# Seven stage joints of one long block: the order of some steps changed

## The chip, the cores and the metric

The kernel runs on one core of one Trainium2 chip. The metric is the time of one execution on the device in microseconds; a kernel is timed in several runs, and their median stands for it. Everything is one program with one launch. One further execution was recorded by the hardware profiler, and all rows below are from it.

## The reference

Two transformer-like blocks on one sequence of 1024 positions and 1024 channels, all in fp32. The first block, cut to what matters:

```python
h = rmsnorm(x, g_mix); z = h @ w_in
a = layernorm(causal_dwconv(a_val * sigmoid(a_gt), 31 taps))   # long branch
y_a = silu(a) @ w_a_out
s = sc_b * causal_dwconv(sc_c * sc_v, 3 taps)                  # short branch
y_b = s @ w_b_out
x = x + (sigmoid(gate_a) * y_a + sigmoid(gate_b) * y_b) @ w_o
u = rmsnorm(x) @ w_up                                          # 2 x 2816 columns
x = x + (gelu(causal_dwconv(u_gate, 3 taps)) * u_value) @ w_down
x = x + sigmoid(rmsnorm(x) @ w_ple_gate) * (p @ w_ple)
```

It ends with a norm. The second block modulates and projects the result again, runs latent attention with four heads and a context of 256 positions, a pooling branch, two gated products and an output projection.

## The kernel before, in words

Activations lie with channels on the 128 partitions and positions along the free axis: a [1024, 1024] activation is eight tiles of 128x1024, each in two halves of 512 columns (h = 0, 1). To hold fp32 accuracy every operand is split into a high and a low part of a shorter format (`split`, `load_w`): ScalarE copies the high part, VectorE or GpSimd subtracts it to get the low part. A product is then three matmuls (`mm3`, lines 138 to 140: high by high, low by high, high by low) that add up in one of eight accumulator banks. `gemm` does this over the input tiles: 24 matmuls for one half of a weight column with eight tiles, 48 for both.

All is written as one straight program; the framework places tiles in pools, inserts the waits and plans the order of each engine's queue, using the program order as priority. So an engine's order is fixed before the run, and may differ from the text. Pools matter here: `slot` has 32 tiles of 128x1024; `half_t` 8 tiles of 128x512; weights have 5 raw buffers and 3 each for high and low; there are 8 banks.

A norm's scale is made in three steps (class `Stats`): squares are added over the tiles; `rstd` sums them over the partitions with small matmuls (line 186) and makes the reciprocal root on VectorE in a chain of small steps, then writes it on the diagonals of four 128x128 blocks (`diag`, line 201); `spread` multiplies a matrix of ones with these diagonals (line 207), which puts the scale on all partitions, and ScalarE copies it out (line 208). TensorE's queue stands at the spread until the diagonal is there.

Stages around the change, in order:

- Short branch. Four tiles `sv` are made and split into `sp_`. Then for each j of 8, `gate(8 + j)` (48 matmuls, two multiplications by the scale `rb` at line 570, a sigmoid), the product "yb" with `w_b_out` (24 matmuls for both halves), a multiplication of the two at line 586, and a store. Between these stand steps of the long branch's convolution, taken from a queue `bgq` by `bg(n)`: it runs up to n steps and stops at a `None`. Then eight more gates follow with `bg(3)` after each half, during which the LayerNorm of the long branch runs from the same queue (`ln_sum`, `ln_mean`, `ln_center`, `ln_sq`, `ln_rstd`, `ln_spread`, `ln_out`).
- Mix and w_o. The loop over h and j of 8 adds the product with `w_o` to x (line 675) and gathers the second norm's squares; for h = 1 it makes the scale of the first half, after j = 2, and spreads it, after j = 4, into `rb2`.
- FFN up. 22 tiles of 128 gate and 128 value columns. Each is made by a scheme of seven products of 12 matmuls (`a0, b0, b1, t1 to t4`) on sums of blocks, instead of eight. `quad_first` does the first tile; `begin(j)` loads the weights of tile j, makes their sums on GpSimd and issues product a0; `quad(j)` does the rest. The result `ug` goes through `ff_conv` (convolution, gelu), is multiplied with the value part in `ff_end` and stored in `f_spill`. The operands of the seven products take 28 slots through all of this.
- FFN down. `load_f` reads a stored tile back and splits it; the 22 tiles come in chunks of 3, 8, 6 and 5 (`FF_CHUNKS`). In the last chunk the loop over h and d of 8 also gathers the third norm's squares; for h = 1 it makes the first half's scale after d = 3 and spreads it into `rb3` after d = 5. Steps of an unrelated matrix-vector product (`mod_step`) run on VectorE from `bgq`.
- PLE. Products "pg" and "ple", the latter with small weights `ws`; the scaled result is split into `hB`.
- Second block. The first gate columns "ga": two weights are loaded, both first halves multiplied, then `norms2(1)` (line 186 sums and a reciprocal root), one second half, `norms2_spread(1)`, the other second half.

## Time and profile before

| | us |
|---|---|
| median of 3 runs | 1999.13 |
| lowest, highest | 1996.34, 2002.65 |
| the profiled execution | 1998.57 |
| its span, first to last instruction | 1996.8 |

How to read what follows: PE is TensorE's matmuls, PEld its weight loads, DVE VectorE, ACT ScalarE, POOL GpSimd, SP the queue of SyncE that issues most DMAs; a "q" behind an engine's name is its queue issuing a DMA. L12 is line 12 of the kernel. An operand is written out<-in by the program's names; a name ending in h or l is a high or low part. The square bracket at the end of a row is the engine's idle time just before and what ended it. A matmul is listed longer than it holds the engine: the next starts before it ends. [...]

### The profile page before, as it was taken

The page shows a single profiled execution, that of the slowest core. Times are in us where ns is not written, and L with a number is a line of the kernel's source. Part 1 is how long each engine was busy: PE and PEld are TensorE (multiplying, and loading weights), DVE is VectorE, ACT ScalarE, POOL GpSimd, SP SyncE. Part 2 cuts the span into 40 slices and gives each one's busy share as a digit, 9 for nine tenths or more (in the row PEclk, how much of TensorE's full clock was granted, in tenths as well). Part 3 has the DMA queues.
Part 4 walks back from the last instruction along what each step waited for, and adds up shares of the span by engine and source line. Part 5 has one row for each costly group of instructions (what it writes and reads, how often), then busy time and mean ns, then how long its engine had stood idle before and what let it go on. Part 6 is the DMA issues. An engine that isn't in the chain of part 4 may idle for free.

```text
span 1996.8 us, 24031 instructions
## 1 busy us (share of the span) xinstructions
PE 1944.2 (97%) x8958; PEld 1581.6 (79%) x8958; DVE 1457.3 (73%) x2219; ACT 705.3 (35%) x1172; POOL 591.1 (30%) x417
## 2 busy tenths in 40 slices
PE   9999989999999999999999999999999999999999
PEld 7888768778877777777777777878778878888887
DVE  6798679356668888888884539986888476878751
ACT  6210221233344333333334322345442256556510
POOL 1334522130012445454541010223354322323200
PEclk9999989999999999999999999999999999999999
DMA  6011122113442222222224535534331221001141
GB/s 216 32 43 38 63 77 76 58 40 108 147 140 89 72 87 70 89 69 90 69 92 166 203 113 191 173 133 147 121 117 55 72 87 35 14 14 43 44 183 48
DMA packets 76612, 186.11 MB, mean 93 GB/s; under 512 B 8784, under 2 KB 15568, under 8 KB 76496
## 3 DMA queue, kind: packets, MB, share of 16 engines
q1 hardware_dynamic: 68000, 162.04, 24.3%
q10 hardware_dynamic: 8496, 22.55, 2.9%
q8 instruction: 70, 1.15, 0.2%
q14 instruction: 46, 0.38, 0.1%
HBM read 149.42 MB, written 35.13 MB: 92 GB/s over the span
## 4 chain that ended last, share of the span: by engine, by line
PE 75%; DVE 12%; issue 6%; ACT 4%; POOL 2%; DMA 1%; ACTq 0%; DVEq 0%; SPq 0%; POOLq 0%
PE q L138 4%; PE wd L139 4%; PE wd L140 4%; PE wd L138 3%; PE q L139 3%; PE q L140 3%; PE gate L139 3%; PE gate L138 3%; PE gate L140 3%; DVE fa L335 2%; PE pv L1338 2%; PE wo L138 2%; PE wout L140 1%; PE wout L139 1%; PE wo L139 1%
## 5 line engine op out<-in xcount | busy, mean ns | idle before, releaser
L133 ACT ACTIVATE wh<-wr 128x1024 fp32r<-128x1024 f32 (+2 forms) x116 | 115.6, 998 | 353.6 <-PE wd L139 90.2
L134 POOL TENSOR_TENSOR wl<-wr,wh 128x1024 fp32r<-128x1024 f32 x44 | 119.8, 2724 | 276.0 <-ACT wh L133 264.4
L156 DVE TENSOR_TENSOR wl<-wr,wh 128x1024 fp32r<-128x1024 f32 (+1 forms) x92 | 159.8, 1737 | 49.7 <-ACT wh L155 49.6
L335 DVE SCALAR_TENSOR_TENSOR acc<-av,vec,acc 128x1023 f32<-128x1023 f32 (+14 forms) x120 | 186.5, 1554 | 10.2 <-ACT acc L344 7.5
L155 ACT ACTIVATE wh<-wr 128x1024 fp32r<-128x1024 f32 (+1 forms) x92 | 86.6, 942 | 205.5 <-issue 137.0
L138 PE MATMUL q<-t,wh 128*128 128x512 f32 x352 | 141.9, 403 | 5.1 <-DVE qm L700 4.7
L139 PE MATMUL wd<-fl,wh 128*128 128x512 f32 x352 | 139.3, 397 | 1.3 <-DVE fl L782 1.2
L139 PE MATMUL q<-t,wh 128*128 128x512 f32 x352 | 139.2, 396 | 0.2 <-DVE t L156 0.2
L140 PE MATMUL q<-t,wl 128*128 128x512 f32 x352 | 139.1, 395 | 0.0
L140 PE MATMUL wd<-fh,wl 128*128 128x512 f32 x352 | 138.5, 395 | 0.0
L138 PE MATMUL wd<-fh,wh 128*128 128x512 f32 x352 | 134.4, 403 | 3.8 <-ACT fh L781 3.8
L225 POOL TENSOR_TENSOR ss<-ss,sq 128x512 f32<-128x512 f32 x42 | 61.8, 1487 | 203.6 <-ACT sq L224 203.6
L138 PE MATMUL gate<-hh,wh 128*128 128x512 f32 x256 | 102.1, 399 | 0.0
L139 PE MATMUL gate<-hl,wh 128*128 128x512 f32 x256 | 101.0, 395 | 0.0
L140 PE MATMUL gate<-hh,wl 128*128 128x512 f32 x256 | 100.5, 393 | 0.0
L134 DVE TENSOR_TENSOR wl<-wr,wh 128x1024 fp32r<-128x1024 f32 (+2 forms) x72 | 83.7, 1162 | 16.4 <-ACT wh L133 15.1
L138 PEld LDWEIGHTS q<-t,wh 128*128 128x128 f32 x352 | 66.3, 188 | 29.2 <-DVE qm L700 13.2
L759 POOL TENSOR_TENSOR fa<-fa,rb 128x1024 f32<-128x1024 f32 x22 | 53.6, 2436 | 120.3 <-ACT fa L758 120.3
L1313 POOL TENSOR_SCALAR wr<-wr,rsum 128x1280 f32<-128x1280 f32 x32 | 42.9, 1341 | 145.8 <-DVE rsum L1312 131.2
L138 PEld LDWEIGHTS wd<-fh,wh 128*128 128x128 f32 x352 | 66.7, 190 | 21.0 <-ACT fh L781 5.1
L139 PEld LDWEIGHTS wd<-fl,wh 128*128 128x128 f32 x352 | 66.6, 189 | 19.2 <-DVE fl L782 3.3
L140 PEld LDWEIGHTS wd<-fh,wl 128*128 128x128 f32 x352 | 66.5, 189 | 15.8
(466 smaller groups left out, 5486.8 us busy)
## 6 DMA issues: line engine op xcount, KB each, us to landing
wr<-in_w_upq SPq DMA_DIRECT2D x88, 256.0 KB, 3.0
wr<-in_w_in SPq DMA_DIRECT2D x32, 512.0 KB, 3.3
wm<-in_w_modT SPq DMA_DIRECT2D x48, 256.0 KB, 3.0
f_spill<-fa ACTq DMA_DIRECT2D x22, 512.0 KB, 2.6
fl<-f_spill SPq DMA_DIRECT2D x22, 512.0 KB, 5.7
x<-in_xT SPq DMA_DIRECT2D x32, 256.0 KB, 4.5
wr<-in_w_o SPq DMA_DIRECT2D x16, 512.0 KB, 3.2
x_spill<-x ACTq DMA_DIRECT2D x32, 256.0 KB, 2.0
```

The costliest lines, as they stand in the source:

```text
L133: S.activation(out=hi, in_=raw, func=AF.Copy)
L134: lo_eng.tensor_tensor(out=lo, in0=raw, in1=f32(hi), op=ALU.subtract)
L138: PE.matmul(ps, lh, rh, start=start, stop=False, **kw)
L139: PE.matmul(ps, lh, rl, start=False, stop=False, **kw)
L140: PE.matmul(ps, ll, rh, start=False, stop=stop, **kw)
L155: S.activation(out=hi, in_=src, func=AF.Copy)
L156: V.tensor_tensor(out=lo, in0=src, in1=f32(hi), op=ALU.subtract)
L225: eng.tensor_tensor(out=self.sums[:, hs(h)], in0=self.sums[:, hs(h)], in1=q, op=ALU.add)
L335: V.scalar_tensor_tensor(out=acc[:, s:T], in0=src[:, 0 : T - s], scalar=w, in1=acc[:, s:T], op0=ALU.mult, op1=ALU.add)
L759: G.tensor_tensor(out=fa, in0=fa, in1=rb2, op=ALU.mult)
L1313: G.tensor_scalar(out=pm, in0=pm, scalar1=rs, scalar2=1.0, op0=ALU.mult, op1=ALU.mult)
L1338: PE.matmul(self.pv, v4[cc][x], y[:, cc, :], start=b + n + cc == 0, stop=b == 4 and n == 2 and cc == 1)
```

## The change

Seven edits, all of order.

- In LayerNorm's part of the queue, `ln_rstd` stands one place earlier: it runs after the half gate that follows the last `ln_sq`, not after the next. `ln_spread` keeps its place.
- `gate(8)` is issued before the loop over j, and each turn issues `gate(9 + j)` before its own product. Products and gates stay the same.
- The spread into `rb2` of the first half moves from after j = 4 to after j = 6.
- The spread into `rb2` of the second half, with the scaling and convolution of FFN tile 0, moves out of the place behind `begin(1)` into a function `first_tile`, which `quad(1)` calls behind its product t2.
- The `load_f` of the first chunk's three tiles stand before the last FFN tile's `quad(21)` instead of after its `ff_end`.
- The spread into `rb3` of the first half moves from after d = 5 to after d = 7.
- At the start of the second block three gate weights are taken instead of two; `norms2(1)` follows three first halves, and its spread two second halves.

```diff
-    bgq.extend([None, ln_rstd, None, ln_spread, None])
+    bgq.extend([ln_rstd, None, None, ln_spread, None])
...
+    ahead = deque([gate(8)])
     for j in range(KD):
-        g = gate(8 + j)
+        if j < KD - 1:
+            ahead.append(gate(9 + j))
+        g = ahead.popleft()
         bg(4)
...
-            if h and j == 4:
+            if h and j == 6:
                 st.spread(rb2, (0,))
...
         product(y, w, "t2")
+        if callable(prev):
+            prev = prev()
         padd(u2, y, m1)
...
-    ug = slot("ug")
-    cs = quad_first(wq0, ug)
+    ug0 = slot("ug")
+    cs0 = quad_first(wq0, ug0)
     nxt = begin(1)
-    st.spread(rb2, (1,))
-    V.tensor_tensor(out=ug, in0=ug, in1=rb2, op=ALU.mult)
-    prev = 0, ff_conv(0, ug), cs
-    for j in range(1, N_FF):
-        ug, cs, nxt = quad(j, *nxt, prev)
-        prev = j, ff_conv(j, ug), cs
-    ff_end(*prev)
+
+    def first_tile():
+        st.spread(rb2, (1,))
+        V.tensor_tensor(out=ug0, in0=ug0, in1=rb2, op=ALU.mult)
+        return 0, ff_conv(0, ug0), cs0
...
+    fs = {}
+    prev = first_tile
+    for j in range(1, N_FF):
+        if j == N_FF - 1:
+            for k in range(FF_CHUNKS[0]):
+                fs[k] = load_f(k)
+        ug, cs, nxt = quad(j, *nxt, prev)
+        prev = j, ff_conv(j, ug), cs
+    ff_end(*prev)
...
         for k in range(j0, j0 + n):
-            fs[k] = load_f(k)
+            if ci:
+                fs[k] = load_f(k)
...
-            if h and d == 5:
+            if h and d == 7:
                 st.spread(rb3, (0,))
...
-    w = [load_w(a["w_fm"][i], KD, lo_eng=G) for i in range(2)]
-    bs = [bias_col(w[i]) for i in range(2)]
-    gs = [[gemm(w[i], hB[0], None, "ga")] for i in range(2)]
+    w = [load_w(a["w_fm"][i], KD, lo_eng=G) for i in range(3)]
+    bs = [bias_col(w[i]) for i in range(3)]
+    gs = [[gemm(w[i], hB[0], None, "ga")] for i in range(3)]
     norms2(1)
     gs[0].append(gemm(w[0], hB[1], None, "ga"))
+    gs[1].append(gemm(w[1], hB[1], None, "ga"))
     norms2_spread(1)
-    gs[1].append(gemm(w[1], hB[1], None, "ga"))
+    gs[2].append(gemm(w[2], hB[1], None, "ga"))
     for i in range(2):
         ga_evict(i, bs[i], gs[i])
-    g = ga_gemm(2)
     next(ctx_parts)
     load_tm(0)
     load_tm(1)
-    ga_evict(2, *g)
+    ga_evict(2, bs[2], gs[2])
```

## Rows read from the trace of the kernel before

**Rows 1.** The page: busy time of TensorE and its weight loads, among all engines.
```profile
PE 1944.2 (97%) x8958; PEld 1581.6 (79%) x8958; DVE 1457.3 (73%) x2219; ACT 705.3 (35%) x1172; POOL 591.1 (30%) x417
```
**Rows 2.** Waits of TensorE: who <- whom: us in total, times, longest.
```profile
PE sp L207 <- DVE dg L201: 10.6, 5, 4.2
PE yb L139 <- DVE spl L156: 5.1, 2, 4.6
...
PE wd L138 <- ACT fh L781: 3.8, 3, 3.1
```
**Rows 3.** Windows: stretch, length, busy (x count) per engine; PEclk, DMA share, GB/s; products yb.
```profile
245.40:263.40 18.00, 9.88 (x26) 6.50 (x25) 15.59 (x14) 2.73 (x3) 6.43 (x3) 0.62 0.05 15
...
274.50:280.10 5.60, 5.60 (x26) 4.55 (x25) 5.53 (x6) 0.93 (x2) 0.00 (x0) 1.00 0.23 94
```
**Rows 4.** Timeline of TensorE at a spread without a wait: start, us, what.
```profile
1353.53 1.02 PE L207 MATMUL sp<-dg,ones 128*128 128x512 f32 x2
1353.98 0.80 PE L138 MATMUL pg<-h,wh 128*128 128x512 f32 x1
1354.62 0.39 PE L139 MATMUL pg<-h,wh 128*128 128x512 f32 x1
```
**Rows 5.** Windows again: stretches around five of the other waits.
```profile
427.70:433.20 5.50, 2.90 (x8) 1.16 (x7) 4.54 (x11) 1.88 (x3) 2.40 (x1) 1.00 0.29 80
595.10:601.20 6.10, 4.11 (x10) 2.32 (x9) 6.10 (x9) 3.20 (x5) 2.10 (x2) 0.72 0.25 72
640.90:648.90 8.00, 3.81 (x8) 2.11 (x7) 7.83 (x13) 0.60 (x1) 5.03 (x4) 0.79 0.03 10
1064.50:1076.00 11.50, 7.50 (x25) 5.09 (x24) 7.50 (x8) 5.72 (x6) 3.29 (x2) 0.85 0.94 338
1312.00:1317.90 5.90, 4.05 (x10) 2.33 (x9) 5.69 (x13) 2.32 (x3) 1.96 (x2) 0.71 0.46 152
```
**Rows 6.** Timeline of VectorE in the short branch.
```profile
256.14 1.23 DVE L156 TENSOR_TENSOR spl<-sv,sph 128x1024 fp32r<-128x1024 f32 x1
...
285.78 0.69 DVE L570 TENSOR_TENSOR gate<-gate,rb 128x512 f32<-128x512 f32 x1 [2.17 <-PE gate L140]
```
**Rows 7.** Timelines of VectorE and TensorE in LayerNorm.
```profile
404.73 0.68 DVE L225 TENSOR_TENSOR lnv<-lnv,sq 128x512 f32<-128x512 f32 x1
...
431.80 1.12 PE L207 MATMUL sp<-dg,ones 128*128 128x512 f32 x2 [2.33 <-DVE dg L201]
```
**Rows 8.** Timeline of VectorE before the second FFN spread.
```profile
641.36 3.96 DVE L201 TENSOR_SCALAR dg<-ident,rc 128x128 f32<-128x128 f32 x4
645.25 0.68 DVE L700 TENSOR_TENSOR ug<-q,qm 128x512 f32<-128x512 f32 x1
```
**Rows 9.** Timelines of TensorE, SyncE's queue and ScalarE at the last FFN tile.
```profile
1053.31 0.50 PE L138 MATMUL q<-t,wh 128*128 128x512 f32 x1 [0.23 <-DVE qm L700]
...
1058.42 0.42 SPq L780 DMA_DIRECT2D fl<-f_spill  x1
...
1066.69 1.04 ACT L781 ACTIVATE fh<-fl 128x1024 fp32r<-128x1024 f32 x1
```
**Rows 10.** Timelines of VectorE and TensorE from the down stage into PLE.
```profile
1320.40 0.69 DVE L855 TENSOR_TENSOR x<-wd,x 128x512 f32<-128x512 f32 x1 [1.67 <-PE wd L140]
...
1330.20 0.75 DVE L134 TENSOR_TENSOR ws<-wr,ws 128x256 fp32r<-128x256 f32 x2
...
1330.66 0.50 PE L140 MATMUL ple<-pp,ws 128*128 128x512 f32 x1 [0.78 <-DVE ws L134]
```
**Rows 11.** Timeline of TensorE at the sums and spread of the second block.
```profile
1458.70 1.84 PE L186 MATMUL ts<-ones,ss 128*128 128x2 f32 x16
...
1466.07 1.02 PE L207 MATMUL sp<-dg,ones 128*128 128x512 f32 x2
```
**Rows 12.** Timelines of ScalarE, VectorE and TensorE: fourth convolution, first and last step, and the mean.
```profile
297.18 1.23 ACT L344 ACTIVATE acc<-av,vec 128x1024 f32<-128x1024 f32 x1
...
351.65 1.25 DVE L335 SCALAR_TENSOR_TENSOR acc<-av,vec,acc 128x994 f32<-128x994 f32 x1
...
391.09 1.02 PE L376 MATMUL mu<-lns,ones 128*128 128x512 f32 x2
```

More of the change, by code (lines that the diff above doesn't have):

```diff
@@ L789, in block_kernel @@
     j0 = 0
-    fs = {}
     def down(d, h, w, n):
```

## The prediction

> **What bounds the kernel now.** I read the page's busy table first: TensorE is busy for 1944.2 of 1996.8 us [rows 1]. No other engine comes near it, so the time can only fall by closing TensorE's idle time, some 50 us with the head and tail, and the slow matmuls right behind it. The second view is who waited for whom on TensorE [rows 2]: the largest entry is the spread of a norm, which waits for VectorE's diagonal (10.6 us in five waits), then the short branch's product and the first product after the FFN. The third view gives each stretch around such a wait its length, its count of instructions and its granted clock [rows 3, 5]. [...] I therefore price a joint as its stretch less its work at full pace. The pace is 24 matmuls in 5.6 us, 0.23 us each [rows 3]. A spread that waits for nothing costs 0.86 us: from its start at 1353.53 to the next full-pace matmul at 1354.62 are 1.09 us, one matmul included [rows 4]. Counts in the windows include one or two instructions that hang over from before.
>
> **The change part by part.** The ceiling of each, and what I take:
>
> 1. Gate one ahead of the short branch. Now the first product takes 18.0 us where a later one takes 5.6 [rows 3], a loss of 12.4. It waits for VectorE's splits, the last ending at 256.14 + 1.23 = 257.4 [rows 6]. The change puts another gate of 48 matmuls (11.1 us) before it, so the product starts near 256.5 and reaches the matmul that needs this split (the tenth or so) at about 258.6: covered with 1.2 us to spare. The second gate's weights are needed earlier; the trace shows no weight wait of a gate, and three weight buffers allow it. VectorE has a backlog until 285.78, where it first waits for TensorE by 2.17 [rows 6]; meanwhile TensorE, 12.4 us ahead, fills banks: two gates, one product and the next gate make at most 7 of 8 by my count, so no new wait. The price, if the splits move later by more than 1.2 us, is one for one. I take 12.0, bounds 8 to 12.4. All gates and products are merely permuted; the gate is stored and read back long after.
>
> 2. LayerNorm's sums half a gate earlier. The stretch of 5.5 us holds two matmuls and two spreads: 5.5 - 0.5 - 1.7 = 3.3, of which 2.33 is the wait before the second spread [rows 5, 7]. The sums move up by half a gate, 5.6 us, more than the wait. Their input is complete at 404.73 + 0.68 [rows 7], long before. I take 3.0, bounds 2.3 to 3.3.
>
> 3. First norm spread of the FFN two weight columns later (j = 4 to 6). 6.1 us hold six matmuls and one spread: 6.1 - 1.4 - 0.9 = 3.8 [rows 5]. Two columns are 48 matmuls, 11.1 us, so the diagonal is ready with margin. But VectorE then feeds the FFN's first tile, and the x loads, queued on SyncE behind weight loads that wait for VectorE, follow no faster than VectorE. I take 3.0, bounds 1.5 to 3.8.
>
> 4. Second spread behind one more product of the second tile. 8.0 us hold five matmuls and a spread: 8.0 - 1.2 - 0.9 = 5.9 [rows 5]. The moved product (12 matmuls, 2.8 us) goes into this wait, but the diagonal still ends at 641.36 + 3.96 = 645.3 [rows 8]. Moreover the product takes the accumulator bank that the spread has now; all eight are in use, and the next is free when VectorE's addition of 645.25 ends at 645.93 [rows 8]. So 2.8 - 0.6 = 2.2 at most return unless the clock stays up, and VectorE's remaining additions may then be waited for. [...]
>
> 5. First three activations reloaded ahead of the last FFN tile. 11.5 us hold 24 matmuls: 11.5 - 5.5 = 6.0 [rows 5]. The first load is issued at 1058.42 and its split on ScalarE starts at 1066.69, while TensorE has run dry [rows 9]. Named earlier, it has room once the products of the last tile give up operand slots, about a tile (20 us) ahead of TensorE's need. On SyncE it passes ahead of the first down weights; these are held by weight buffers anyhow. Against it: three ScalarE copies and three VectorE subtractions enter the last tile's queues, where TensorE already waits 0.23 us for an addition [rows 9]. If a subtraction of 1.2 us (128x1024, as the split of 256.14 [rows 6]) stands ahead of that addition, TensorE pays it. I take 5.0, one such collision; bounds 2 (three collisions) to 6.0.
>
> 6. Spread after the down product two rows later (d = 5 to 7). 5.9 - 1.4 - 0.9 = 3.6 [rows 5]. Here VectorE is the next bound. Right behind, TensorE waits 0.78 us for the small weights' lower part, which VectorE makes at 1330.20 at the end of a queue with only 1.67 us of idle time at 1320.40 [rows 10]. TensorE comes 3.6 earlier, VectorE can follow by 1.7, so this wait grows by 1.9. I take 3.6 - 1.9 = 1.7, bounds 0 to 3.6.
>
> 7. Third gate weight ahead in the second block. The sums at 1458.70 and the spread at 1466.07 show no idle time before them [rows 11]: nothing waits where the change adds cover. The waits just before are for the previous stage's last splits, which all three first halves still need. One more weight's bias column comes forward on VectorE. I take 0, bounds -1.5 to +1.
>
> Sum: 12.0 + 3.0 + 3.0 + 1.8 + 5.0 + 1.7 + 0 = 26.5. The profiled execution took 1998.57 (span 1996.8), 0.6 below the median of 1999.13; 1998.6 - 26.5 = 1972.1. No instruction is removed or added; all of it is order.
>
> **The rivals.**
>
> A. Every wait closes, and the clock with it: 12.4 + 3.3 + 3.8 + 5.9 + 6.0 + 3.6 = 35.0, giving 1963.6. For it: each edit sits at a measured wait. Against it: parts 4 and 6 have VectorE close behind.
>
> B. The next-late resource takes the place of the waits: parts 3 to 6 return nothing on balance, because diagonals, splits and additions all hang on VectorE; parts 1 and 2 hold: 15.0, giving 1983.6. For it: the diagonal of part 4 and the queue of part 6. Against it: parts 3 and 5 have microseconds of cover.
>
> C. The change does not do what it says. The framework orders each engine's queue by a plan of its own, and reorders across the program text: the reload of part 5 already stands ahead of the last tile's end [rows 9]. The plan may already issue what the text moves, or put the moved work back. Then the waits stay: 1993 to 2002, about 1998.
>
> D. Slower, by one mechanism: tile room. The pool has 32 slots; at the short branch I count 16 for the normalised input, 1 scale, 3 accumulators, 1 or 2 inputs, 8 for the branch's splits, leaving 2 or 3 for gates and the fourth accumulator. The change keeps two gates alive where one was. The fourth convolution starts at 297.18, its last step ends at 352.9, and TensorE needs the resulting mean at 391.09 [rows 12], which becomes 378.7. With three sums of 1.2 us, 22 us are spare. If the second gate held the accumulator's slot until the branch's splits go free (the last product, at 262 + 6 x 11.1 + 7 x 5.6 = 368), the convolution would start 71 us later, TensorE would stand for 71 - 22 = 49, and the time would be 1972 + 49 = 2021. It decides the sign once the start slips beyond about 347. Against it: two slots suffice for two gates, and VectorE's lag, not room, sets the start.
> [...]
>
> **How the numbers follow.** Forecast (1968 to 1980): 0.50. B and mixtures towards it: 0.25. A: 0.12. C: 0.08. D: 0.05. The likeliest time is 1972. The lower bounds of all parts together save 13, the upper ones 36; a range from 1962 to 1987 takes in forecast, A and B, and leaves out C, D and a few hundredths of tails. About 0.3% (6 us) is what a measurement here can tell from no change; faster by more is forecast, A and B together, 0.87; within it is C, 0.08; slower is D, 0.05.
>
> **What would show it.** In the changed profile: the first short-branch product takes about 5.6 us, at clock 1.00; no spread in LayerNorm, FFN entry j or down stage has a wait before it except the second FFN spread, with 1.5 to 2; the first product after the FFN follows the last tile at once; the small-weight wait near the first PLE product grows from 0.8 to nearly 3; nothing changes at the second block's start. The prediction is wrong if a wait of several us stands in the last FFN tile (loads not landed), before the LayerNorm mean (slots), or if the attention stage's order, untouched by the text, comes out otherwise.

## The result, and the profile after

The changed kernel takes 1976.7 us (median of four runs, 1974.2 to 1980.3) against 1999.0 of the kernel before beside it; the ratio is 0.9889, with a 95% interval of 0.9875 to 0.9904. Run again later beside other kernels it took 1979.5 us (1977.3 to 1980.3), a ratio of 0.9898 [0.9883, 0.9913]. The profiled execution took 1974.2 us with a span of 1972.4, 24.4 below the one of before. The forecast was 1972, with a range of 1962 to 1987.

The page of the changed kernel, busy time of all engines, answers to [rows 1]:

```profile
PE 1935.7 (98%) x8958; PEld 1578.8 (80%) x8958; DVE 1457.4 (74%) x2219; ACT 705.9 (36%) x1172; POOL 593.2 (30%) x417
```

The counts are the same as before: nothing was added. TensorE is busy 8.5 us less with the same work, as less of it falls in stretches of a lower granted clock (PEclk, a share of full speed, is 0.997 over the whole span, where it was 0.992; single microseconds of the changed kernel read 1.00 from 1294 to 1300 us and 0.50 from 1301 to 1306). The waits of TensorE in the changed kernel (who <- whom: us in total, times, longest), beside [rows 2]:

```profile
PE q L138 <- DVE qm L703: 7.3, 20, 1.8
...
PE ple L140 <- DVE ws L134: 3.0, 2, 2.3
...
PE ple L138 <- ACT ws L133: 2.6, 1, 2.6
PE sp L207 <- DVE dg L201: 2.3, 1, 2.3
...
PE q L139 <- DVE t L156: 1.0, 2, 0.8
...
PE q L138 <- ACT wh L155: 0.8, 1, 0.8
```

The 10.6 us at spreads have become 2.3, and these are at another spread, the context's at 1482.10. The waits of the short branch's product and of the first down product are gone. New or larger are the small weight of the per-layer embedding (ple), the FFN's additions (qm), among which now stands one of 1.8 us, and the splits for the FFN's first products (t, wh).

To see where the time went I take the start of the same matmul in both traces and compare the lengths of the stretches between. "Again" is the second profile of the changed kernel. Matmuls are counted from 0 among those of one output: wo for the output projection, q for the FFN, wd for its down product, pg for the PLE gate (PLE is the per-layer embedding). All in us; a minus is time lost.

| stretch | before | after | again | saved: after (again) | predicted |
|---|---|---|---|---|---|
| start to the first gate | 234.25 | 234.59 | 234.60 | -0.3 (-0.4) | 0 |
| to LayerNorm's mean | 156.84 | 144.39 | 144.39 | 12.5 (12.5) | 12.0, part 1 |
| to the output projection (matmul 190) | 174.94 | 171.80 | 171.80 | 3.1 (3.1) | 3.0, part 2 |
| to the first FFN matmul | 50.72 | 46.86 | 46.86 | 3.9 (3.9) | with the next |
| to FFN matmul 300 (fourth tile) | 79.07 | 78.27 | 80.25 | 0.8 (-1.2) | 4.8, parts 3 and 4 |
| to FFN matmul 1740 | 343.16 | 343.11 | 343.14 | 0 (0) | 0 |
| to down matmul 60 | 45.60 | 39.92 | 39.92 | 5.7 (5.7) | 5.0, part 5 |
| to down matmul 1024 | 227.08 | 224.22 | 225.69 | 2.9 (1.4) | 0 |
| to PLE gate matmul 48 | 27.81 | 29.65 | 28.36 | -1.8 (-0.6) | 1.7, part 6 |
| to the token-major products (utm) | 208.94 | 210.62 | 212.18 | -1.7 (-3.2) | 0, part 7 |
| to the end | 448.36 | 449.00 | 451.29 | -0.6 (-2.9) | 0 |
| sum, unrounded | | | | 24.4 (18.3) | 26.5 |

Two profiles of one kernel are 6 us apart, and yet half of the rows agree to 0.03 us. So a whole execution says little about an edit worth 2 us; its stretch says much, if it is one of the steady ones. The experiments below are read that way.

Three joints as they stand now. Windows of the changed kernel (stretch, length, busy per engine with counts, granted clock, DMA share, GB/s), the first product of the short branch:

```profile
256.80:262.50 5.70, 5.70 (x26) 4.65 (x25) 5.62 (x6) 1.26 (x3) 0.00 (x0) 1.00 0.00 0
```

It takes 5.7 us at a granted clock of 1.00 where it took 18.0 at 0.62 [rows 3]. Timelines of TensorE, VectorE and GpSimd around the second FFN spread (start, us, what; in brackets idle time before it):

```profile
622.70 0.88 DVE L201 TENSOR_SCALAR dg<-ident,rc 128x128 f32<-128x128 f32 x4
...
627.21 1.02 PE L207 MATMUL sp<-dg,ones 128*128 128x512 f32 x2
...
626.04 1.29 POOL L652 TENSOR_TENSOR wr<-wr 128x512 f32<-128x512 f32 x1 [17.44 <-DVE wl L156]
```

The diagonal of four steps took 3.96 us before [rows 8] and takes 0.88 now. Before, GpSimd's weight additions ran beside it, from 641.35 to beyond its end, 1.3 us each; now they come 2.5 us after it. Timeline of GpSimd before:

```profile
641.35 1.26 POOL L649 TENSOR_TENSOR wr<-wr 128x512 f32<-128x512 f32 x1 [15.76 <-DVE rc L180]
```

The spread has no wait. Timeline of TensorE at the end of the FFN: the first down product follows the last FFN product with no gap, and the last tile's wait is 0.60 us, where 0.23 was normal [rows 9]:

```profile
1033.74 0.50 PE L138 MATMUL q<-t,wh 128*128 128x512 f32 x1 [0.60 <-DVE qm L703]
...
1044.74 0.39 PE L140 MATMUL q<-t,wl 128*128 128x512 f32 x1
1044.97 0.40 PE L138 MATMUL wd<-fh,wh 128*128 128x512 f32 x1
```

### The profile page after: what moved, and what is told of

The parts are those of the page before. It is cut to its first block, busy times and chain, and to the rows that moved or that the text cites. A ratio compares the mean times of both kernels' runs of the same rounds, so it can differ in the third digit from the quotient of the medians.

```text
span 1972.4 us, 24045 instructions
## 1 busy us (share of the span) xinstructions
PE 1935.7 (98%) x8958; PEld 1578.8 (80%) x8958; DVE 1457.4 (74%) x2219; ACT 705.9 (36%) x1172; POOL 593.2 (30%) x417
## 4 chain that ended last, share of the span: by engine, by line
PE 43%; DVE 12%; issue 5%; ACT 4%; POOL 1%; DMA 1%; DVEq 0%; SPq 0%; ACTq 0%; POOLq 0%
PE q L138 3%; PE wd L139 3%; PE wd L140 3%; PE wd L138 3%; PE q L140 3%; PE q L139 3%; DVE fa L335 2%; PE pv L1351 2%; PE wout L138 2%; PE wout L140 2%; PE wout L139 1%; PE pg L138 1%; PE pg L140 1%; PE pg L139 1%; PE pT L1340 1%
## 5 line engine op out<-in xcount | busy, mean ns | idle before, releaser
L138 PEld LDWEIGHTS q<-t,wh 128*128 128x128 f32 x352 | 66.0, 188 | 33.1 <-DVE qm L703 16.5
L139 PEld LDWEIGHTS q<-t,wh 128*128 128x128 f32 x352 | 66.1, 188 | 16.9 <-DVE t L156 1.9
```

The lines of the kernel that those rows point to most:

```text
L138: PE.matmul(ps, lh, rh, start=start, stop=False, **kw)
L139: PE.matmul(ps, lh, rl, start=False, stop=False, **kw)
```

## The experiments

Unless said otherwise the diffs are against the changed kernel, and a run is one profiled execution. The names of the second block: ga are its gate products; pin the products of its pooling branch (the expectations call them pinned); between these stand the parts of the context, which are its sums, its spread, its product uc (with the low part hcl) and a transposition ckTc; utm are the token-major products, kv the first products of the attention.

**The first part alone.** The kernel before, with only the gate drawn ahead.

```diff
+    ahead = deque([gate(8)])
     for j in range(KD):
-        g = gate(8 + j)
+        if j < KD - 1:
+            ahead.append(gate(9 + j))
+        g = ahead.popleft()
```

> The kernel before with the first of the edits alone: one gate ahead of the short branch's product. Theory (the wait was for VectorE's splits, and nothing downstream gives the time back): the first product takes 5.7 us instead of 18.0, TensorE reaches the LayerNorm mean 12.4 us earlier than before, and the whole is 12.4 +- 1 shorter than the kernel before (profiled span near 1984.4). Rival (two gates alive take tile room, later stages absorb part): under 9 us at the end, with a wait in the long branch's convolution or at the mean.

It took 1988.1 us (span 1986.3). From the first gate to the mean it needs 144.39 us, the same to 0.01 as the whole change: 12.45 us are this part's alone. The stretches to the FFN are as before (174.95, 50.75). The span is 10.5 shorter than that of before, which neither theory named: 1.0 us is lost ahead of down matmul 60, and 2.2 us at the context's first product, in a stretch that no edit touches, by a wait that the trace of before does not have:

```profile
PE uc L140 <- DVE hcl L520: 1.8, 1, 1.8
```

**The third part undone** (first FFN spread back at column 4).

```diff
-            if h and j == 6:
+            if h and j == 4:
                 st.spread(rb2, (0,))
```

> The changed kernel with the FFN's first spread put back after j = 4. Theory 1 (the start of the FFN is paced by VectorE's chain of differences, splits and additions, so that the two spread edits share one limit): the spread waits some 2 us again, TensorE enters the FFN 3.8 us later, but by the fourth FFN tile only 0 to 2 us of that are left, and the end is 0 to 2 later than the changed kernel (span 1972.4 to 1974.5). Theory 2 (the edits add up): 3.8 later at the fourth tile and at the end, span 1976.2.

It took 1977.2 us. The entry to the FFN is 50.71 us again, as before (50.72). From the output projection to FFN matmul 300 it needs 128.8 us; the ten profiles with both parts need 125.1 (the changed kernel's first) to 127.4, so the part is worth 1.4 to 3.7 us there, 2.6 by their mean. At the end the run is 3.05 us behind the first profile and 3.0 ahead of the second. That does not decide between theory 1 (0 to 2 us left) and theory 2 (3.8). The spreads of this run wait so:

```profile
PE sp L207 <- DVE dg L201: 4.2, 2, 2.3
...
PE sp L207 <- DVE ug L703: 1.9, 1, 1.9
```

The second line is the second FFN spread waiting for the accumulator bank, the wait that the prediction expected of part 4. It stands only where the third part is missing. The diagonal ahead of it stood beside GpSimd's weight additions again and took 4.00 us, as before. Timelines of VectorE and GpSimd:

```profile
625.87 4.00 DVE L201 TENSOR_SCALAR dg<-ident,rc 128x128 f32<-128x128 f32 x4
...
626.02 1.29 POOL L652 TENSOR_TENSOR wr<-wr 128x512 f32<-128x512 f32 x1 [15.89 <-DMA wr<-in_w_upq]
```

**The fourth part undone** (second spread and first tile ahead of the second tile again).

```diff
-        if callable(prev):
-            prev = prev()
...
-    def first_tile():
-        st.spread(rb2, (1,))
...
+    st.spread(rb2, (1,))
...
```

> The changed kernel with the second FFN spread and the rest of tile 0 back behind product a0 of tile 1. Theory 1 (in the changed kernel the diagonals took 0.9 us, beside an idle GpSimd, instead of 4.0 beside its additions; and the tiles after are paced by VectorE): the spread waits 0 to 2 us, and at the fourth FFN tile TensorE is 0 to 2 us later than in the changed kernel. Theory 2 (the moved product's cover is what closed this wait): 4 to 6 us of wait and slow clock return, and 3 or more are left at the fourth tile and at the end (span 1975.4 or more).

It took 1976.8 us. To FFN matmul 300 it is 1.8 us behind the changed kernel, as theory 1 has it, but 0.6 of that lies ahead of the moved piece, where runs scatter; from matmul 84 to 150 it needs 17.4 us against 16.2 to 16.3 in the ten profiles with both parts. The second spread has no wait here either. So with the third part in place it is not the spread that the fourth part shortens: the moved tile saves 1.1 us, most of it one wait of 0.97 us for an addition. By matmul 300 nothing of it can be told any more: from the output projection this run needs 126.9 us, inside the 125.1 to 127.4 of the ten.

**The fifth part undone** (activations of the first down chunk reloaded behind the last tile).

```diff
-        if j == N_FF - 1:
-            for k in range(FF_CHUNKS[0]):
-                fs[k] = load_f(k)
...
-            if ci:
-                fs[k] = load_f(k)
+            fs[k] = load_f(k)
```

> The changed kernel with its fifth part alone undone: the activations of the first down chunk are reloaded behind the last FFN tile again. Theory 1: the part is worth what the lead showed at the first down products: a wait on the first reloaded activations at the start of the down stage comes back (3.8 us in two waits in the kernel before) with the slow clock behind it, and the stretch from the fourth FFN tile's first product to the 60th down product is 5.7 us longer than in the changed kernel (5.0 to 6.3); the whole is 5 to 7 us longer. Theory 2: the reload ahead of the tile also moves the later chunks' loads: then the waits at the later chunk borders (near 1104 and 1198 in the kernel before, 0.7 us of lead) come back as well, and the down stage's pace goes back from 233.0 to 234.9 ns a product, so that about 2.5 us more are gone by the end of the down stage (8 us in all). Theory 1 keeps the pace at 233 ns.

From FFN matmul 1740 to down matmul 60 it needs 45.67 us (before 45.60, with the part 39.92): the part is worth 5.7 us, and the wait is back:

```profile
PE wd L138 <- ACT fh L784: 3.1, 1, 3.1
```

The whole took 1986.7 us, 12.5 more than the first profile of the changed kernel and 6.4 more than the second (1980.3). So the size of theory 1 is right for the border. Of theory 2 something may be right too: the rest of the down stage needs 226.1 us here, 226.7 and 227.1 in the two other profiles without the part, and 224.2 to 225.7 (mean 225.0) in the eleven with it. The two sets do not overlap, so the part probably saves a further 1.1 to 1.6 us there; with three profiles on one side, of which only this one differs by the part alone, that is not shown.

**The sixth part undone** (down-stage spread back at row 5).

```diff
-            if h and d == 7:
+            if h and d == 5:
                 st.spread(rb3, (0,))
```

> The changed kernel with the spread of the third norm put back after d = 5. Theory 1 (VectorE is late at the end of the down stage, so what the moved spread saves is lost at the small weights of the first PLE product): the spread waits 1.5 to 2 us again, the wait at the small weights falls from 3.4 to about 0.8 us, and the time from the last down product's start to the second PLE weight column is the same within 1 us; span 1971.5 to 1973.5. Theory 2 (the late small weights have another cause): both waits stand, and the span is 3 to 4 us longer, near 1976.

It took 1974.2 us, the same as the changed kernel's first profile, though it lost 1.3 us between FFN matmuls 150 and 300, where the clock was lower (0.92 from 673.67 to 695.27). The spread waits 2.10 us and the small weight 0.77, as theory 1 has it. The stretch into the embedding is 26.45 us. With the part it was 29.65, 28.36, 26.67, 29.20, 28.38, 29.10 and 28.67 in seven profiles, and without it 27.81 in the kernel before and 28.16 in the run of the first part alone. The part is worth nothing, or less: theory 1, with more lost than it said.

**The first small weight earlier.** If VectorE's queue makes the embedding's first small weight late, it must help to load and split it ahead of the rush.

```diff
                 st.rstd(D, (0,))
                 load_pp(0)
+                ws = load_w(a["w_ple"][0], 2)
...
-    ws = load_w(a["w_ple"][0], 2)
     for h in range(2):
```

> The changed kernel with the first small weight of the per-layer embedding loaded and split earlier: behind the down stage's fourth output of the second half instead of behind its last. In the changed kernel its two halves are waited for 2.63 us (the high part, ScalarE) and 0.73 us (the low part, VectorE), and the stretch from the last down product to pg48 is 29.65 us. Theory 1, place in the queues: ScalarE reaches the split only behind its wait for VectorE's last down eviction; with the split ahead of it the two waits of the first ple product are 0.5 us or less, the clock stays at the upper level, and the stretch is 26 us (25.5 to 27), 3 to 4 us under the changed kernel. Theory 2, VectorE is simply full between 1268 and 1303: the wait moves to the next product that VectorE feeds (the following weight, or the evictions' banks), and the stretch stays at 28.5 us or more.

The stretch is 23.07 us, 6.6 less than in the first profile of the changed kernel and below the 25.5 to 27 of theory 1; it holds 99 matmuls, 0.233 us each, and no wait. Theory 1 took off the two waits, 3.36 us; the other 3.2 are the lower clock behind them (0.90 over the 23 us, against 1.00). Windows of the same 23 us, the changed kernel first, then this one, from the profile of the timed run below:

```profile
1281.50:1304.50 23.00, 19.64 (x75) 14.65 (x74) 21.83 (x42) 11.97 (x19) 6.08 (x4) 0.90 0.38 129
```
```profile
1281.50:1304.50 23.00, 23.00 (x99) 18.27 (x98) 20.98 (x41) 12.10 (x20) 7.12 (x5) 1.00 0.42 131
```

VectorE has as much to do in both (21.8 and 21.0 us). It was not too slow; one short operation stood too late. The whole was timed in more runs:

> The changed kernel with the first small weight of the per-layer embedding loaded behind the down stage's fourth output of the second half. In one look the stretch from the last down chunk's first product to pg48 was 23.1 us against 29.65 of the changed kernel, and no wait stood from 1260 to 1310. Theory 1: these 6.6 us reach the end but for what the VectorE-bound stretch from 1400 to 1500 us takes back (1 to 2 us), so the median is 4 to 6 us under the changed kernel's. Theory 2: the later stretch takes most of it, as the one look seems to say (1972.7 us, 1.5 under the changed kernel's profile, 1.8 of the difference lost by chance in the FFN); the median is 0 to 3 us under it.

1972.2 us (1970.5 to 1973.8), ratio 0.9863 [0.9846, 0.9879]; the changed kernel beside it took 1979.5, and none of its eight runs (1974.2 to 1980.3) lies among these. The difference of 7.3 is more than theory 1 gave; against the changed kernel's earlier median of 1976.7 it is 4.5. This version is the fastest of the study.

**The changed kernel again.**

> The changed kernel once more, unedited, beside the two that follow. Theory 1: the 22.3 us between the first medians are the change; the median is 1976 us (1974 to 1979) and the ratio to the kernel before 0.988 to 0.990. Theory 2, a lucky pairing of runs that scatter by 3 us from one to the next: the ratio is above 0.991. In the trace the six places where it waits (651.5, 673.0, 1299.8, 1301.6, 1415.6, 1482.1 us in the first profile) stand again within 0.3 us of their sizes.

1979.5 us, half a microsecond above theory 1's band, and a ratio of 0.9898, inside it; theory 2 falls, by the median (the interval ends at 0.9913). The waits stand where they stood (0.87, 1.77, 2.18, 1.03, 2.26, 2.24 us); the third is 0.45 shorter and the fourth 0.3 longer than in the first profile. What differs more is the clock behind them. Windows of FFN matmuls 204 to 288 and 288 to 372, one tile's work each, in the first profile, then the same two of this one:

```profile
651.40:673.02 21.62, 19.78 (x85) 15.63 (x85) 16.60 (x16) 6.38 (x7) 12.82 (x8) 1.00 0.22 73
673.02:693.03 20.01, 19.78 (x84) 15.69 (x84) 17.14 (x15) 6.38 (x7) 10.00 (x7) 1.00 0.24 79
```
```profile
651.90:673.45 21.55, 19.78 (x84) 15.62 (x85) 16.53 (x15) 6.38 (x7) 12.75 (x8) 1.00 0.22 73
673.45:695.04 21.59, 21.36 (x85) 16.85 (x85) 17.19 (x15) 6.39 (x7) 9.98 (x7) 0.92 0.24 74
```

In both profiles the first window ends in the same wait of 1.77 us; behind it the next 84 matmuls take 20.01 us at a granted clock of 1.00 in one execution and 21.59 at 0.92 in the other. That is 1.6 us of the 6 by which the two profiles differ.

**The seventh part undone** (two gate weights ahead instead of three).

```diff
-    gs = [[gemm(w[i], hB[0], None, "ga")] for i in range(3)]
...
+    gs = [[gemm(w[i], hB[0], None, "ga")] for i in range(2)]
...
+    norms2_spread(1)
     gs[1].append(gemm(w[1], hB[1], None, "ga"))
-    norms2_spread(1)
-    gs[2].append(gemm(w[2], hB[1], None, "ga"))
...
+    g = ga_gemm(2)
...
```

> The changed kernel with its seventh part alone undone: two gate weights of the last block are loaded ahead of the first normalization again, and the third product starts behind the second spread. In the changed kernel this part cut the two hB waits and the slow clock behind them (2.5 us of lead gained by the 73rd ga product), but the context's spread at 1482.1 then waited 2.27 us and the pinned matmuls 0.35 us (3.1 us of lead lost by pin48), net 1.2 us lost. Theory 1, the order costs it: without the part the context's spread stands without a wait again, the hB waits come back (0.9 and 1.4 us in the kernel before), and from the first ga product to pin48 the run takes 1.2 us less than the changed kernel (0.5 to 2.0). Theory 2, jitter of that stretch: the spread of the context waits here too (2 us or so), and the stretch from ga0 to pin48 is 2 to 3 us longer than in the changed kernel.

The pooling branch's first 48 matmuls (pin) take 11.80 us (14.91 with the part), the context's spread does not wait where it waited 2.27 us, and the stretch named is 2.4 us shorter: theory 1, and more than its 0.5 to 2.0. But the stretch ends too early. Behind it stands a new wait:

```profile
PE uc L140 <- DVE hcl L520: 2.4, 1, 2.4
```

From PLE gate matmul 360 to the token-major products it needs 117.9 us; with the part 116.3 to 118.0 in the six profiles whose context code is as in the changed kernel and whose small weights stand where it has them, 114.6 in the kernel before and 116.1 in the first part alone. The part is worth nothing that can be told from the scatter.

**The context's third part a column later.**

```diff
-        next(ctx_parts, None)
+        if i:
+            next(ctx_parts, None)
```

> The changed kernel with the third part of the context (its spread among it) issued one column of pinned products later. In the changed kernel the spread of the context waits 2.27 us on VectorE's diagonal at 1482.1, and pin0 to pin48 loses 3.1 us of lead. Theory 1: the third part comes too early for VectorE since the third gate product was moved ahead of it; a column later the diagonal is done, the wait at the spread is under 0.3 us, and the stretch from ga0 to pin48 is 2 to 3 us shorter than in the changed kernel. Theory 2: VectorE's own queue holds the diagonal, in whose order the column's evictions come first as well: the spread waits as long as before a column later (1.5 us or more), and the stretch is the same within 1 us.

The spread no longer waits, the first 48 pin matmuls take 12.18 us, and the stretch named is 3.2 us shorter: theory 1. But a wait of the same size appears at the context's last step, and from PLE gate matmul 360 to the first kv product the run needs 213.2 us, between the two profiles of the changed kernel (210.8 and 214.5). Nothing is gained:

```profile
PE ckTc L537 <- DVE uc L490: 2.4, 1, 2.4
```

**Small weights two ahead** in the embedding's second half, on top of the early first one. In every profile so far the last of them was waited for 2.25 us.

```diff
...
+            if h and d == 4:
+                wsq.append(load_w(a["w_ple"][5], 2))
+            nxt_w = d + 2 if h and d >= 4 else d + 1
...
```

> As the run before, and in the second half of the per-layer embedding the small weights are loaded two products ahead from the fifth on: the last of them was waited for 2.25 us (its low part on VectorE) in every profile so far. Theory 1, place in VectorE's queue: the wait at the last ple product is under 0.3 us, the first ga product starts 2.3 us earlier, and the end is 1 to 3 us earlier than in the run before. Theory 2, VectorE is full there (23.2 of 25.0 us busy from 1400 to 1425, 34.8 of 35.0 from 1465 to 1500): the wait moves to hB or to the context's spread, the stretch from pg360 to kv0 is within 1 us of the run before, and so is the median.

The wait is gone and the next block's first product starts 2.5 us sooner in its stretch. Then TensorE waits for the normalised activations: 1.04, 3.25 and 0.84 us. Timelines of ScalarE, VectorE and GpSimd in this run:

```profile
1414.66 0.63 ACT L224 ACTIVATE sq<-x 128x512 f32<-128x512 f32 x1 [4.02 <-DVE x L926]
...
1411.27 2.39 DVE L159 SCALAR_TENSOR_TENSOR hB<-x,amul,hB 128x512 fp32r<-128x512 f32 x1
...
1410.72 2.39 POOL L134 TENSOR_TENSOR wl<-wr,wh 128x1024 fp32r<-128x1024 f32 x1 [0.53 <-ACT wh L133]
```

ScalarE, which makes the activations, stands 4.02 us for VectorE's addition, and that is behind a subtraction of 2.39 us (0.73 at 1403.57) beside a GpSimd operation of the same length. From PLE gate matmul 360 to the first kv product the run needs 217.0 us, 4.6 more than without the edit; the median is 1974.5 (1971.2 to 1976.6) against 1972.2 (1970.5 to 1973.8): the two sets of runs overlap, so the whole alone would not tell. Theory 2's direction held, and the price in the stretch was higher than it said; its reason, that VectorE is full, is not borne out: from 1406 to 1424 VectorE is busy for 13.97 of the 18 us, and for 16.21 without the edit.

**The context's root earlier**, again on top of the early small weight.

```diff
-    g = ga_gemm(3)
     next(ctx_parts)
+    g = ga_gemm(3)
```

> The changed kernel with the first small embedding weight loaded early (as timed before, 1972.2 us) and the context's inverse root issued ahead of the fourth gate product instead of behind it. In the run before it the token sums of the context were ready at 1466.0 us and VectorE took them up at 1475.9, behind bias steps of which several take 2.4 us instead of 0.3; the spread then waited 2.23 us and the matmuls behind it ran at a lower clock (pin0 to pin48 14.99 us against 11.82 in the kernel before). Theory 1, place in VectorE's queue: the diagonal is written before 1472, the spread has no wait, pin0 to pin48 is 11.9 us, and from pg360 to the first kv product the run takes 209 to 210 us (212.4 and 212.0 without the edit), so the median is about 1969.5 us. Theory 2, VectorE is full there whatever the order: the wait goes on to the context's next product (uc, on its low part hcl, 2.4 us, as where the third gate product was put back), the stretch is within 1 us of 212, and the median is 1971 to 1974 us.

The diagonal is written at 1462.5, the spread does not wait, and the first 48 pin matmuls take 12.58 us instead of 14.99. (The expectation speaks of a lower clock behind the spread in the run without the edit. The spread stands at the end of these matmuls, and the 48 after it have a granted clock of 1.00 there: the 14.99 us hold the spread's wait of 2.23 us and one of 0.46 for a weight.) The next product of the context then waits:

```profile
PE uc L140 <- DVE hcl L520: 3.9, 1, 3.9
```

From PLE gate matmul 360 to the first kv product it needs 216.6 us, against 212.4 without the edit, and the median is 1975.4 (1974.8 to 1976.5). The wait moved on, as theory 2 says, and grew; stretch and median lie above theory 2's figures too. Timelines of VectorE and GpSimd show some 2 us of it, first the run without the edit, then with it; L959 is a bias step, hcl what TensorE waits for:

```profile
1491.75 1.86 DVE L1050 TENSOR_TENSOR edge<-pw,cinv 128x1 f32<-128x1 f32 x1
1493.54 0.28 DVE L959 TENSOR_SCALAR wr<-wr,mod 128x128 f32<-128x128 f32 x1
1493.73 0.87 DVE L520 SCALAR_TENSOR_TENSOR hcl<-cx,mod,hch 128x256 fp32r<-128x256 f32 x2
...
1493.73 4.55 POOL L134 TENSOR_TENSOR wl<-wr,wh 128x1024 fp32r<-128x1024 f32 x1
```
```profile
1491.70 1.87 DVE L1050 TENSOR_TENSOR edge<-pw,cinv 128x1 f32<-128x1 f32 x1
1493.48 2.44 DVE L959 TENSOR_SCALAR wr<-wr,mod 128x128 f32<-128x128 f32 x1
1495.85 0.87 DVE L520 SCALAR_TENSOR_TENSOR hcl<-cx,mod,hch 128x256 fp32r<-128x256 f32 x2
...
1493.51 2.34 POOL L134 TENSOR_TENSOR wl<-wr,wh 128x1024 fp32r<-128x1024 f32 x1
```

The same operations stand in the same order, and up to the bias step they start within 0.06 us of each other. Where GpSimd's subtraction came 0.19 us after the bias step, the step took 0.28 us and GpSimd's 4.55; where it came 0.03 us after it, the step took 2.44 and GpSimd's 2.34. The queue position of an operation is thus one part of the matter here; another is what GpSimd begins beside it.

## Why the prediction was right, and where its steps failed

The forecast of 1972 was 4.7 below the first median and 2.2 below the profiled execution; the sum of 26.5 met 24.4, or 18.3 in the second profile. That it came so close is owed to the large terms. The small ones missed in both directions, and that they cancelled in the first profile is luck. The upper bounds of the parts, with 4.6 for part 4, add up to 34.7, not to 36 as the text on the range says; no conclusion hangs on it.

**Part 1** was taken at 12.0 and measured 12.45, in every run with it. Its steps stand in the trace: the product begins at 256.80, and no bank is waited for behind it. Rival D, the room for tiles, is refuted: the LayerNorm mean starts 12.1 us earlier than before, with no wait ahead of it. (One wait of the trace before repeats, that for the FFN's additions, 19 times and 0.3 us at most. It names VectorE, not room.)

**Part 2** was taken at 3.0 and measured 3.14, as the stretch less its work at pace said. No run undoes it alone, but it is the only edit in its stretch, and the run of the first part alone needs 174.95 us there, as before.

**Part 5** was taken at 5.0 and measured 5.7. The step that was mis-sized is the collision: one subtraction ahead of the last tile's addition was priced at 1.2 us, and the wait grew by 0.37 only. The ceiling by window of 6.0 was the better estimate.

**Parts 3 and 4** were taken at 4.8 together and measured 4.7 in the first profile, 2.7 in the second, 2.4 to 4.7 in the ten with both; the agreement hides two errors. The 1.8 for part 4 in the sum was my choice between 0.5 and 4.6, and no run shows it: the part undone cost 1.1 us between FFN matmuls 84 and 150 and nothing that can be told by matmul 300. The step on the diagonal failed: it was to end 3.96 us after its start as before, and a wait of 1.5 to 2 us was to stay. With TensorE 3.9 us earlier at the FFN the diagonal ran before GpSimd's additions, took 0.88, and the wait went altogether; with the third part undone it ran beside them and took 4.00. So both ceilings came back whole, 3.9 us at the entry and 5.9 between FFN matmuls 84 and 150 (22.16 us before, 16.26 now). Then half of this was lost again, where the sum had next to nothing. Matmuls 0 to 84 take 23.99 us instead of 21.58, with waits of 0.77 and 0.82 us for splits of VectorE and ScalarE. From 150 to 300 another 2.7 us go: the sentence that "VectorE's remaining additions may then be waited for" came true, larger than the 0.4 us that the sum left for it, with 0.86 us at matmul 204, 1.77 at 288, and in four profiles a lower clock behind that (0.92). GpSimd and VectorE ahead of matmul 288 of the changed kernel:

```profile
668.85 2.43 POOL L764 TENSOR_TENSOR fa<-fa,rb 128x1024 f32<-128x1024 f32 x1 [5.14 <-ACT fa L763]
...
669.75 2.60 DVE L156 TENSOR_TENSOR wl<-wr,wh 128x1024 fp32r<-128x1024 f32 x1 [1.53 <-ACT wh L155]
672.29 0.68 DVE L703 TENSOR_TENSOR qm<-q,qm 128x512 f32<-128x512 f32 x1
```

The addition that TensorE waits for stands behind a weight split of 2.60 us, whose like, at 648.97, takes 1.22 where GpSimd is idle. Behind matmul 288 each tile takes 20.0 us, as before, 19.8 of them TensorE's. That VectorE and GpSimd set the rhythm of the FFN's loop, so that a head start cannot last there, is my reading, and no run shows it: in the window from 673.02 shown above VectorE is busy for 17.1 of the 20.0 us and GpSimd for 10.0.

**Part 6** is where a step failed in sign. It was taken at 1.7: TensorE 3.6 us earlier, VectorE able to follow by the 1.67 us for which it had stood idle [rows 10], the rest a longer wait for the small weight's lower part. Measured: a loss of 1.8 in the first profile, 0.9 by the median of the seven, 2.2 by that median against the run with the part undone. The waits are 2.63 and 0.73 us where 0.78 was [rows 10]: they grew by 2.6, not 1.9, and the lower clock behind them, which the sum put at nothing, cost some 3.2 us more (the stretch is 29.65 us, 23.07 without either; the clock is 0.90 in the window above). Timelines of the changed kernel, ScalarE, then VectorE:

```profile
1297.76 0.72 ACT L158 ACTIVATE h<-x,vec 128x512 fp32r<-128x512 f32 x1 [4.18 <-DVE x L868]
...
1299.38 1.02 ACT L133 ACTIVATE ws<-wr 128x256 fp32r<-128x256 f32 x3
...
1294.05 1.78 DVE L446 SCALAR_TENSOR_TENSOR mj<-wm,cb 128x512 f32<-128x512 f32 x1
...
1297.04 0.68 DVE L868 TENSOR_TENSOR x<-wd,x 128x512 f32<-128x512 f32 x1
...
1301.14 0.75 DVE L134 TENSOR_TENSOR ws<-wr,ws 128x256 fp32r<-128x256 f32 x2
```

I had followed VectorE alone. The weight's upper part is ScalarE's, and ScalarE reaches it only after it has stood 4.18 us for VectorE's last eviction, which VectorE does at 1297.04 behind background steps (mj) of up to 1.78 us. Here a queue that follows another pays its own delay and the other's. The run with the small weight loaded early shows that this place is the cause: all 6.6 us came back.

**Part 7** was taken at 0 with bounds of -1.5 to +1. Its stretch lost 1.7 and 3.2 us in the two profiles, outside these bounds, but not by this part as far as the runs tell: the first part alone loses 1.7 there too, and undoing the seventh part brings nothing back. What does cost it stays open. The two waits for the last splits shrank to one of 0.94 us, and the context's spread then waited 2.27 us, which was not foreseen. Three edits that removed a wait in this stretch (the seventh part undone, the context a column later, the root earlier) each brought up another behind it, of 2.4 to 3.9 us.

**Not predicted:** 1.4 to 2.9 us saved within the down stage, where no edit is. Some 1.1 to 1.6 of them probably belong to part 5, going by the three profiles without it. Two waits at the later chunk borders, 0.43 and 0.30 us in the kernel before, come and go; which loads of later chunks move, and why the stretch scatters by 1.5 us among kernels with the part, stays open.

Of the rivals, A was right at parts 1, 2 and 5 and wrong where VectorE was close; B was right about part 6, half right about 3 and 4, and wrong about 5; C fell with the first part, since the plan did issue what the text moved.

## What to carry to other kernels

A joint's price is its stretch less its work at full pace (the small weight's was 6.6 us, with waits of 3.36), and here three of the seven parts (1, 2 and 5), each with microseconds of cover, returned nearly all of theirs, 21 of the 24 us. Where the next engine is within 2 us, follow every queue that stands between it and the waiting one (here VectorE to ScalarE to TensorE), and look for the short operation that stands late rather than for a way to give the busy engine less; measure from ahead of the joint to behind the next three waits, since the waits that three edits removed in the second block's stretch came up again behind it, with 2.4 to 3.9 us. Judge an edit of 2 us by a stretch that repeats to 0.1 us, not by whole executions that scatter by 6.

## What the runs showed of the hardware

**Bias steps of VectorE took 0.3 us, and 2.4 beside a split of GpSimd.** Timelines of GpSimd and VectorE in the changed kernel: three splits of GpSimd, 2.42 us each, and beside them three bias steps of VectorE of 128x128, whose medians in this run are 0.28 us (L959) and 0.35 (L961):

```profile
1466.41 7.26 POOL L134 TENSOR_TENSOR wl<-wr,wh 128x1024 fp32r<-128x1024 f32 x3 [3.90 <-ACT wh L133]
...
1466.52 4.89 DVE L961 SCALAR_TENSOR_TENSOR wr<-wr,mod 128x128 f32<-128x128 f32 x2
1471.34 2.42 DVE L959 TENSOR_SCALAR wr<-wr,mod 128x128 f32<-128x128 f32 x1
1473.68 0.60 DVE L961 SCALAR_TENSOR_TENSOR wr<-wr,mod 128x128 f32<-128x128 f32 x2
```

Each of the three steps lasts as long as one of GpSimd's operations (2.4 us), and the next two, after GpSimd is done, 0.3 each. In the two runs compared at the context's root one bias step took 0.28 us where GpSimd's subtraction started 0.19 us after it and 2.44 where it started 0.03 us after it; GpSimd's subtraction took 4.55 and 2.34. What decides between the two outcomes no run shows. I had priced VectorE's operations by their durations in the trace of before (3.96 us for the diagonal) as if these were the operations' own.

**The clock behind a wait is not settled by the wait.** After the same 1.8 us of idle time at FFN matmul 288 the granted clock of the next 84 matmuls was 0.92 in four profiles, and they took 21.6 us; in seven others they took 20.0, at 1.00 in the one shown above. The context's spread waited 2.2 us in nine profiles. Behind it TensorE's work from pin matmul 48 to 96, with the context's product, took 17.0 us at a granted clock of 1.00 in five of them and 18.6 to 19.5 us in four. Windows of this work in the first profile of the changed kernel and in the second:

```profile
1482.75:1499.78 17.03, 17.03 (x101) 14.92 (x100) 16.92 (x30) 5.08 (x11) 9.53 (x3) 1.00 0.12 32
```
```profile
1485.15:1503.74 18.59, 18.59 (x101) 16.07 (x100) 18.41 (x35) 5.09 (x11) 7.96 (x3) 0.91 0.14 43
```

So one and the same wait cost its own length in some executions and 1.5 us or more on top in others.
